# A dilated convolution on one core: all transfers on one hardware queue, no dummy matmuls, first load in halves, last stores in quarters

## The chip, the core and the metric

One core of a Trainium2 chip (trn2). The metric is the device time of the kernel in microseconds (us), as a median over several executions. Before: 127.46 us (127.44 to 127.64, 3 runs). Every ratio below compares a kernel with the kernel before, on one chip with runs of both in turn. Where two variants are set side by side, they often ran on different chips, so their ratios to before are the fairer comparison. The profiled execution of one run has its own span, which is about 1.8 us shorter than the device time (125.6 of 127.34 us before).

## The reference

A 3x3 convolution with dilation 2 over 16 images of 64 channels and 64 by 64 points, 128 output channels, all float32:

```python
batch, c_in, h, w, c_out, k, dilation = 16, 64, 64, 64, 128, 3, 2
# x_pad: zeros of width 2 around each image
for b, co, ci, kh, kw in ...:
    output[b, co] += weight[co, ci, kh, kw] * x_pad[b, ci, kh*2:kh*2+64, kw*2:kw*2+64]
```

The input is 16.8 MB, the output 33.6 MB, the weights 0.3 MB. All of it must cross between HBM and the core once.

## The kernel before

Images are handled in eight pairs (two images of 64 channels fill 128 partitions). A pair is loaded in one 2 MB transfer, cast to fp16 by ScalarE, and convolved in four groups of 16 rows. A group is 30 matmuls in three products (psP, psA, psB); ScalarE copies psP, VectorE adds it to psA and psB and writes the output tile `osb`. Each image of a pair is stored in one 2 MB transfer; those of the first and last pair in halves of 1 MB. Four input buffers and three output buffers rotate.

```python
    x32pool = ctx.enter_context(tc.tile_pool(name="x32pool", bufs=XB))     # XB = 4
    opool = ctx.enter_context(tc.tile_pool(name="opool", bufs=3))
    # ... cut
    def load(pb, rows):
        t = x32pool.tile([P, HW], f32, tag="x32", name="x32")
        x32_tiles[pb] = t
        lo = 0
        for hi in rows:
            nc.sync.dma_start(out=t[:, lo * W : hi * W], in_=x_pair[pb, :, lo * W : hi * W])
            lo = hi
    # ... cut
    def store(pb, m, lo, hi):
        queue = nc.gpsimd if pb < npairs - 1 else nc.sync
        queue.dma_start(
            out=out_img[2 * pb + m, :, lo * W : hi * W],
            in_=o_tiles[pb][:, m * HW + lo * W : m * HW + hi * W],
        )
    # ... cut
    nc.sync.dma_start(out=w32, in_=weight.rearrange("o i h w -> o (i h w)"))
    for pb in range(min(XB, npairs)):
        load(pb, [H])
    # ... cut
    run_warm(14)          # 14 dummy matmuls of 512 columns
    # ... weights: cast to wd (DVE, ACT), 15 transposes (PE), copies to w_sb (DVE, ACT)
    run_warm(14)
    # ... cut; at the end of group G = (pair pb, quarter g):
        if ahead[0] >= NG * (freed[0] + 1) and freed[0] + XB < npairs:
            load(freed[0] + XB, [H])
            freed[0] += 1
        if pb in (0, npairs - 1) and g % 2 == 1:
            for m in range(2):
                store(pb, m, (g - 1) * GR, (g + 1) * GR)
        elif 0 < pb < npairs - 1 and g == NG - 1:
            for m in range(2):
                store(pb, m, 0, H)
```

GpSimd's transfers (`nc.gpsimd`) go through the software queue, SyncE's (`nc.sync`) and ScalarE's through a hardware queue each.

## Time and profile before

| | before |
|---|---|
| device time, median | 127.46 us |
| span of the profiled execution | 125.6 us |
| TensorE (PE) dense | 10.47 to 110.5 us |
| last eviction ends (VectorE) | 111.87 us |
| last transfer fully landed | 124.48 us |
| 16 KB packet on a DMA engine, median | 611 ns |

First the page of the kernel before. In part 2, each of the 40 columns is a fortieth of the span and a digit is the busy share in tenths; in part 3, a line is a queue with its packets, megabytes and share of the 16 DMA engines' time.

```profile
span 125.6 us, 2342 instructions
...
PE   6998999999999999999979999999999999920000
...
DMA  5999999999999999999999999999999999999970
GB/s 160 383 444 418 438 423 402 381 415 444 391 457 418 410 418 436 441 444 418 423 423 425 428 449 423 428 418 423 428 449 423 428 428 418 412 431 407 428 331 16
...
q0 software_dynamic: 2304, 29.36, 55.1%
q1 hardware_dynamic: 1872, 21.27, 40.8%
q8 instruction: 8, 0.13, 0.4%
```

The DMA row is full from the second slice to the 38th. TensorE's last digit, a 2, is in slice 36, and the transfers go on into slice 39. DMA is the bound. The last slices are worth a look: 331, then 16 GB/s. Not all engines end together.

The next lines are the waits of the kernel before: engine and line, what it waited for, total us, times, longest.

```profile
DVE osb L224 <- PE psA L167: 11.7, 25, 1.1
DVE osb L224 <- DMA out_dram<-osb: 3.1, 2, 2.7
```

VectorE waited for matmuls in general, but twice, once for 2.7 us, for a store to free an output buffer. So TensorE runs ahead and DMA holds it back. The timeline of PE at the start (start, duration, work, count) shows where the dummy matmuls stand:

```profile
1.19 5.08 PE L125 MATMUL wp<-warm 128*128 128x512 f16 x14 [1.19 <-DVE warm L120]
6.11 1.00 PE L147 MATMUL wt<-ident,wd 128*128 128x128 f16 x15
6.95 3.19 PE L125 MATMUL wp<-warm 128*128 128x512 f16 x14
10.47 0.81 PE L167 MATMUL psP<-xs,w_sb 64*128 64x512 f16 x6 [0.34 <-DVE xs L98]
11.12 1.28 PE L167 MATMUL psA<-x_157,w_sb 64*128 64x512 f16 x12
...
13.49 0.80 PE L167 MATMUL psP<-xs,w_sb 64*128 64x512 f16 x6
```

The first 14 dummies take 5.08 us, the second 3.19 us: within the first set the spacing drops from 0.43 to 0.216 us at 5.0 us. The prediction reads this as TensorE's clock warming; the granted clock of that stretch is printed as 1.00 and does not show it. Last, the table of stretches of the kernel before (stretch, its length, busy time and instruction counts of PE, weight loads, DVE, ACT, POOL, then granted clock, DMA share, GB/s):

```profile
18.00:20.00 2.00, 2.00 (x22) 0.91 (x20) 1.52 (x3) 1.51 (x2) 1.20 (x2) 1.00 0.96 410
20.00:22.00 2.00, 2.00 (x22) 0.92 (x20) 1.54 (x3) 1.27 (x2) 0.00 (x0) 1.00 1.19 410
22.00:24.00 2.00, 2.00 (x24) 1.02 (x22) 1.99 (x3) 1.79 (x3) 0.00 (x0) 1.00 0.86 348
...
40.00:100.00 60.00, 59.27 (x578) 30.43 (x576) 50.98 (x58) 37.22 (x39) 4.21 (x8) 1.00 1.01 428
```

The rate is a steady 428 GB/s, except for a dip (410, then 348 GB/s).

### The profile page before, as it was taken

Reading aid. Unit: us, or ns where it says so; the run is one execution under the profiler, and the core shown is the slowest. Engines: PE = TensorE matmul, PEld = TensorE weight load, DVE = VectorE, ACT = ScalarE, POOL = GpSimd, SP = SyncE. Lnnn points to the kernel's source line nnn. Section 1 sums busy time; section 2 is a strip of 40 time slices with the busy share of each in tenths; the row PEclk is TensorE's granted clock in tenths of the full one; section 3 lists DMA queues with packets and bytes.
Section 4 is the critical chain, followed back from the end, with each engine's and each line's share of the span. In section 5 each row is a group of like instructions: output and inputs, shape, how many; then the busy total and the mean of one; then the engine's idle time right before and its main releaser. Section 6 shows DMA issues by size and latency. Waiting matters only on the chain.

```text
span 125.6 us, 2342 instructions
## 1 busy us (share of the span) xinstructions
PE 108.3 (86%) x1003; PEld 53.8 (43%) x1003; DVE 89.9 (72%) x105; ACT 66.9 (53%) x71; POOL 9.3 (7%) x22
## 2 busy tenths in 40 slices
PE   6998999999999999999979999999999999920000
PEld 2453444544454445444435555555555555500000
DVE  0732888988898888988649998889888988760000
ACT  4558686966666666666654666666666433300000
POOL 2000003030002001100210003000200120000000
PEclk9999999999999999999999999999999999997555
DMA  5999999999999999999999999999999999999970
GB/s 160 383 444 418 438 423 402 381 415 444 391 457 418 410 418 436 441 444 418 423 423 425 428 449 423 428 418 423 428 449 423 428 428 418 412 431 407 428 331 16
DMA packets 4186, 50.78 MB, mean 404 GB/s; under 512 B 464, under 2 KB 464, under 8 KB 592
## 3 DMA queue, kind: packets, MB, share of 16 engines
q0 software_dynamic: 2304, 29.36, 55.1%
q1 hardware_dynamic: 1872, 21.27, 40.8%
q8 instruction: 8, 0.13, 0.4%
q14 instruction: 2, 0.02, 0.0%
HBM read 17.07 MB, written 33.55 MB: 403 GB/s over the span
## 4 chain that ended last, share of the span: by engine, by line
PE 54%; DMA 27%; DVE 4%; DVEq 1%; ACT 1%; issue 1%; POOL 0%; SPq 0%
PE psA L167 22%; DMA out_dram<-osb 21%; PE psB L167 21%; PE psP L167 11%; DMA x_80<-in_x_dram 6%; DVE osb L224 4%; ACT x_157 L88 1%; DVEq L274 1%; DVE xs L98 1%; POOL out_dram L102 0%; SPq L111 0%; DVEq L224 0%
## 5 line engine op out<-in xcount | busy, mean ns | idle before, releaser
L167 PEld LDWEIGHTS <-w_sb 64*128 64x128 f16 x960 | 49.9, 94 | 50.6 <-issue 1.0
L220 ACT COPY p_sb<-psP 128x1024 f32<-128x1024 f32 x32 | 32.4, 1012 | 37.7 <-PE psP L167 18.2
L224 DVE TENSOR_TENSOR osb<-psA,p_sb 128x1024 f32<-128x1024 f32 x32 | 39.2, 1224 | 15.2 <-PE psA L167 11.7
L224 DVE TENSOR_TENSOR osb<-psB,p_sb 128x1024 f32<-128x1024 f32 x32 | 39.0, 1218 | 0.0
L167 PE MATMUL psP<-xs,w_sb 64*128 64x496 f16 (+1 forms) x192 | 25.7, 371 | 0.3 <-DVE xs L98 0.3
L102 POOL DMA_DIRECT2D out_dram<-osb x16 | 8.6, 540 | 91.3 <-DVE osb L224 91.3
L125 PE MATMUL wp<-warm 128*128 128x512 f16 x28 | 8.3, 460 | 1.2 <-DVE warm L120 1.2
L167 PE MATMUL psB<-x_695,w_sb 64*128 64x496 f16 (+3 forms) x48 | 5.6, 365 | 0.7 <-DVE osb L224 0.7
L167 PE MATMUL psB<-x_1017,w_sb 64*128 64x496 f16 (+3 forms) x48 | 5.6, 365 | 0.0
L167 PE MATMUL psB<-x_856,w_sb 64*128 64x496 f16 (+3 forms) x48 | 5.6, 365 | 0.0
L167 PE MATMUL psB<-x_1178,w_sb 64*128 64x496 f16 (+3 forms) x48 | 5.6, 365 | 0.0
L167 PE MATMUL psA<-x_1178,w_sb 64*128 64x496 f16 (+3 forms) x48 | 5.6, 365 | 0.0
L167 PE MATMUL psA<-x_1017,w_sb 64*128 64x496 f16 (+3 forms) x48 | 5.6, 365 | 0.0
L167 PE MATMUL psA<-x_856,w_sb 64*128 64x496 f16 (+3 forms) x48 | 5.6, 365 | 0.0
L167 PE MATMUL psA<-x_695,w_sb 64*128 64x496 f16 (+3 forms) x48 | 5.6, 365 | 0.0
L167 PE MATMUL psA<-x_157,w_sb 64*128 64x496 f16 (+3 forms) x48 | 5.6, 365 | 0.0
L167 PE MATMUL psA<-x_240,w_sb 64*128 64x496 f16 (+3 forms) x48 | 5.6, 365 | 0.0
L167 PE MATMUL psA<-x_532,w_sb 64*128 64x496 f16 (+3 forms) x48 | 5.6, 365 | 0.0
L167 PE MATMUL psA<-x_369,w_sb 64*128 64x496 f16 (+3 forms) x48 | 5.6, 365 | 0.0
L167 PE MATMUL psB<-x_240,w_sb 64*128 64x496 f16 (+3 forms) x48 | 5.6, 365 | 0.0
L167 PE MATMUL psB<-x_157,w_sb 64*128 64x496 f16 (+3 forms) x48 | 5.6, 365 | 0.0
L167 PE MATMUL psB<-x_369,w_sb 64*128 64x496 f16 (+3 forms) x48 | 5.6, 365 | 0.0
(35 smaller groups left out, 66.3 us busy)
## 6 DMA issues: line engine op xcount, KB each, us to landing
out_dram<-osb POOLq DMA_DIRECT2D x12, 2048.0 KB, 17.6
out_dram<-osb POOLq DMA_DIRECT2D x4, 1024.0 KB, 20.8
out_dram<-osb SPq DMA_DIRECT2D x4, 1024.0 KB, 11.8
x_80<-in_x_dram SPq DMA_DIRECT2D x1, 2048.0 KB, 7.6
x_82<-in_x_dram SPq DMA_DIRECT2D x1, 2048.0 KB, 12.0
x_84<-in_x_dram SPq DMA_DIRECT2D x1, 2048.0 KB, 17.9
x_86<-in_x_dram SPq DMA_DIRECT2D x1, 2048.0 KB, 23.8
x_245<-in_x_dram SPq DMA_DIRECT2D x1, 2048.0 KB, 17.5
```

Source lines behind the costliest of these rows:

```text
L88: nc.scalar.copy(out=x16_tiles[pb][:, lo * W : hi * W], in_=x32_tiles[pb][:, lo * W : hi * W])
L98: nc.vector.tensor_tensor(out=s, in0=v[:, :, 0], in1=v[:, :, 1], op=add)
L102: queue.dma_start(out=out_img[2 * pb + m, :, lo * W : hi * W], in_=o_tiles[pb][:, m * HW + lo * W : m * HW + hi * W],)
L125: nc.tensor.matmul(out=wp[:, 0:512], lhsT=warm[:, 0:P], rhs=warm)
L167: nc.tensor.matmul(out=po, lhsT=w_sb[pp, t * CO : (t + 1) * CO], rhs=rhs, start=first and j == 1, stop=last and j == 2,)
L220: nc.scalar.copy(out=p_sb, in_=psP)
L224: nc.vector.tensor_tensor(out=o[:, :, b0 : b0 + NBLK, e], in0=ps.rearrange("p (m b q) -> p m b q", m=2, q=2 * W), in1=pv, op=add,)
L274: with _tile.TileContext(nc) as tc:
```

## The change

The intent: one kind of queue, with transfers in the order of the program; no work on TensorE that isn't needed; an earlier start of the first cast; a shorter last transfer.

```diff
     def store(pb, m, lo, hi):
-        queue = nc.gpsimd if pb < npairs - 1 else nc.sync
-        queue.dma_start(
+        nc.sync.dma_start(
 ...
     for pb in range(min(XB, npairs)):
-        load(pb, [H])
+        load(pb, [H] if pb else [32 + d, H])
 ...
-    warm = wpool.tile([P, 512], f16, name="warm")
-    nc.vector.memset(warm, 0.0)
-    (definition of run_warm cut)
-    run_warm(14)
 ...
-    run_warm(14)
 ...
-        if pb in (0, npairs - 1) and g % 2 == 1:
+        if pb == npairs - 1 and g == NG - 1:
+            for m in range(2):
+                for lo in (2 * GR, 3 * GR):
+                    store(pb, m, lo, lo + GR)
+        elif pb in (0, npairs - 1) and g % 2 == 1:
```

More of the change, by code (lines that the diff above doesn't have):

```diff
@@ L112 @@
     for pb in range(min(XB, npairs)):
-        load(pb, [H])
+        load(pb, [H] if pb else [32 + d, H])
     ident = wpool.tile([P, P], f16, name="ident")
     make_identity(nc, ident)
-    warm = wpool.tile([P, 512], f16, name="warm")
-    nc.vector.memset(warm, 0.0)
-    wp = ppool.tile([P, 1024], f32, tag="p", name="wp")
-    def run_warm(n):
-        for _ in range(n):
-            nc.tensor.matmul(out=wp[:, 0:512], lhsT=warm[:, 0:P], rhs=warm)
-    run_warm(14)
     KINDS = 5
```

## The prediction

> **What bounds it now.** The DMA engines. The page's DMA row shows 9 in 37 of 40 slices; the table of stretches gives 428 GB/s from 40 to 100 us. 17.07 MB read plus 33.55 MB written at that rate is 118 us (estimate) of the 125.6 us span. TensorE is dense from 10.47 to 110.5 us, a group of 30 matmuls every 3.17 us. The chain of waits calls PE 54%, but at 64.4 us VectorE has waited 2.67 us for a store to free an output buffer: PE is ahead and DMA holds it back.
>
> Landings differ by engine: of the last store half the increments had come at 122.5 us, the last at 124.48. The instruction queue fetches 8 packets of 16 KB, one per 13 us; I think all on one engine. It moves (50.62/16 + 0.131) MB; at 611 ns per 16 KB this is 122.9 us (estimate), from its first packet at 1.74 us to 124.6: never idle, the true bound.
>
> **What the change does.**
> 1. *Stores to the hardware queue.* The Trainium skill ("DMA: Bandwidth & Descriptors", "Issuing engines are not separate DMA queues") says queues share the same 16 engines; the trace agrees: 426 GB/s with the hardware queue alone (9 to 18.7 us), 428 with the software queue alone (80 to 100 us). No gain in rate. Order changes to first in, first out: pair 1's stores land near 58 us, not 64.4, and the output-buffer wait (0.9 us of PE) disappears.
> 2. *No dummy matmuls.* 28 matmuls, 8.3 us of PE, all in its free time. But they warm the clock: the first ran at 0.43 us spacing until 5.0 us, the second 14 at 0.228. The skill ("TensorE: Matmul & The Clock Gate", Part 1) puts the half clock at the first 3.4 us of activity; this trace shows about 3.8. Now transposes run cold (1.6 us, not 1.0), and the first 4 to 5 us of real matmuls cost double: PE about 2.4 us late (1.7 to 3.5). Net of step 1, PE's work ends about 113.4 instead of 111.9.
> 3. *Half first load.* Lands near 6 us instead of 8.78, but the cast follows ScalarE's weight copies, which now end near 8.9. Worth nothing.
> 4. *Quarter stores.* One goes 3.2 us earlier, behind work still queued. Nothing.
> 5. PE's program is 56 instructions shorter: at 256 per fetch, the fetch at 111.47 us should not occur: 0.6 us less for the slowest engine.
>
> **Critical path.** Does PE's lateness starve DMA? At 100.1 us, when pair 6's stores are issued, the preceding store still needs 2.8 us on the median engine, 4.5 on the slowest. 1.5 us later plus 1 us to first data just fits: median engines idle 0 to 1 us, the slowest never. So only the 0.6 us reaches the end.
>
> **Prediction: 126.9 us, range 125.6 to 128.6.** Faster by over 2%: 0.06; within 2%: 0.88; slower: 0.06.
>
> **What would show it.** DMA row 9 throughout; first real matmuls at doubled spacing until about 15 us; first group near 10.6; no long wait of VectorE for stores; last eviction near 113.4; 7 instruction fetches; last landing near 123.9.
>
> **What would make it wrong.** The clock staying low longer, so that DMA idles before pair 6's stores (slower); alternation of two queues itself costing time (348 GB/s at 22 to 24 us, as the software queue starts), so that one queue saves 1 to 2 us; the hardware queue blocking its issuer (its two-store issues took 1.25 and 1.90 us).

## The result, and the profile after

The changed kernel took 127.63 us (median of 6 runs, 127.56 to 127.70), the kernel before 127.45 us in the same rounds. The ratio is 1.0013, 95% interval 1.0000 to 1.0026. (Ratios here are the mean time of one kernel's fast runs over that of the other's of the same rounds, so not quite the ratio of the medians.) Executions over 1.5% slower than the fastest of the same kernel are left out of the means. The time lies inside the predicted range and within 2%, but the gain of 0.6 us that was forecast did not come; if anything, 0.2 us were lost.

The page of the changed kernel:

```profile
span 125.8 us, 2289 instructions
...
PE   0519999999999999999999999999999999930000
...
DMA  4999999999999999999999999999999999999980
GB/s 135 391 458 432 417 427 432 443 284 414 453 427 396 450 424 417 432 435 437 406 422 427 424 443 427 417 432 432 427 437 427 422 417 427 448 409 411 413 326 35
...
q1 hardware_dynamic: 4608, 50.63, 96.2%
q8 instruction: 7, 0.11, 0.3%
```

One queue, still full throughout, and seven instruction fetches instead of eight, as forecast. VectorE's waits in the changed kernel:

```profile
DVE osb L211 <- PE psA L155: 14.4, 26, 2.9
DVE osb L211 <- ACT p_sb L207: 1.6, 5, 0.6
DVE osb L211 <- PE psB L155: 0.4, 1, 0.4
```

These are all of its waits at the eviction: there is none for a store any more. The start of PE in the changed kernel:

```profile
4.39 0.50 PE L135 MATMUL wt<-ident,wd 128*128 128x128 f16 x3 [4.39 <-DVE wd L123]
5.21 1.65 PE L135 MATMUL wt<-ident,wd 128*128 128x128 f16 x12 [0.32 <-DVE wd L126]
9.63 1.43 PE L155 MATMUL psP<-xs,w_sb 64*128 64x512 f16 x6 [2.78 <-DVE xs L98]
10.84 2.42 PE L155 MATMUL psA<-x_127,w_sb 64*128 64x512 f16 x12
13.03 2.24 PE L155 MATMUL psB<-x_127,w_sb 64*128 64x512 f16 x12
15.10 0.81 PE L155 MATMUL psP<-xs,w_sb 64*128 64x512 f16 x6
```

The real work begins 0.84 us earlier than before, its first group is slow (1.43, 2.42 and 2.24 us for the three products; later ones take 0.81, 1.44 and 1.44), and the second group starts 1.6 us later than before (15.10 against 13.49). The last eviction ends at 112.57 us, 0.7 us later than before. The stretches of the changed kernel:

```profile
24.00:26.00 2.00, 2.00 (x24) 1.16 (x22) 2.00 (x3) 1.79 (x3) 0.00 (x0) 1.00 1.01 418
26.00:28.00 2.00, 2.00 (x24) 1.08 (x20) 1.83 (x4) 1.40 (x2) 0.00 (x0) 1.00 1.04 270
28.00:30.00 2.00, 2.00 (x22) 0.96 (x18) 1.52 (x3) 1.65 (x2) 0.00 (x0) 1.00 0.86 352
...
40.00:100.00 60.00, 60.00 (x585) 31.20 (x582) 52.15 (x60) 37.52 (x39) 0.00 (x0) 1.00 1.01 428
```

The same 428 GB/s from 40 to 100 us; the dip has moved to 26 to 30 us and is deeper.

No view above tells why the end did not move. A finer reading does. The Trainium skill ("DMA: Bandwidth & Descriptors", "Why a DMA increments its semaphore by 16 and not by 1") says that each of the 16 engines adds one to the semaphore when its own share has landed. The trace keeps the time of each of these 16 updates, so for each transfer it shows when the median engine was done and when the last one was. I worked out the following from those times (us from the start of the span; "late" is the last engine minus the median):

```
                                first store of pair 2       last store
kernel                          median   last   late      median    last   late
before                           67.80  69.22   1.43      122.51  124.48   1.98
after                            67.95  70.97   3.01      122.61  125.02   2.41
```

The median engine is the same to 0.15 us in both kernels. What differs is how late the last engine is, and in both it is about two us late at the end. So the question is what makes single engines late.

### The profile page after: what moved, and what is told of

Same layout as the page of the kernel before. It is cut to its first block, busy times and chain, and to the rows that moved or that the text cites. A ratio compares the mean times of both kernels' runs of the same rounds, so it can differ in the third digit from the quotient of the medians.

```text
span 125.8 us, 2289 instructions
## 1 busy us (share of the span) xinstructions
PE 103.7 (82%) x975; PEld 53.7 (43%) x975; DVE 90.0 (72%) x104; ACT 66.9 (53%) x71; POOL 0.7 (1%) x6
## 4 chain that ended last, share of the span: by engine, by line
PE 81%; DVE 3%; DMA 2%; ACT 1%; DVEq 1%; issue 0%
PE psA L155 32%; PE psB L155 31%; PE psP L155 17%; DMA w_78<-in_weight_dram 2%; PE wt L135 1%; DVE osb L211 1%; DVEq L265 1%; ACT x_127 L88 1%; DVE wd L126 1%; DVE wd L123 1%; ACT w_sb L142 0%; DVE w_sb L141 0%; DVE xs L98 0%; DVEq L211 0%
## 5 line engine op out<-in xcount | busy, mean ns | idle before, releaser
L155 PEld LDWEIGHTS <-w_sb 64*128 64x128 f16 x960 | 52.3, 95 | 51.9 <-issue 5.2
L155 PE MATMUL psP<-xs,w_sb 64*128 64x496 f16 (+1 forms) x192 | 26.5, 379 | 2.8 <-DVE xs L98 2.8
L155 PE MATMUL psA<-x_127,w_sb 64*128 64x496 f16 (+3 forms) x48 | 6.7, 420 | 0.0
L155 PE MATMUL psB<-x_127,w_sb 64*128 64x496 f16 (+3 forms) x48 | 6.4, 403 | 0.0
L135 PE MATMUL wt<-ident,wd 128*128 128x128 f16 x15 | 2.1, 308 | 4.7 <-DVE wd L123 4.4
L155 PE MATMUL psB<-x_339,w_sb 64*128 64x496 f16 (+3 forms) x48 | 5.6, 365 | 0.0
L155 PE MATMUL psB<-x_502,w_sb 64*128 64x496 f16 (+3 forms) x48 | 5.6, 365 | 0.0
L155 PE MATMUL psB<-x_826,w_sb 64*128 64x496 f16 (+3 forms) x48 | 5.6, 365 | 0.0
L155 PE MATMUL psB<-x_210,w_sb 64*128 64x496 f16 (+3 forms) x48 | 5.6, 365 | 0.0
L155 PE MATMUL psB<-x_665,w_sb 64*128 64x496 f16 (+3 forms) x48 | 5.6, 365 | 0.0
L155 PE MATMUL psB<-x_987,w_sb 64*128 64x496 f16 (+3 forms) x48 | 5.6, 365 | 0.0
L155 PE MATMUL psB<-x_1148,w_sb 64*128 64x496 f16 (+3 forms) x48 | 5.6, 365 | 0.0
L155 PE MATMUL psA<-x_339,w_sb 64*128 64x496 f16 (+3 forms) x48 | 5.6, 365 | 0.0
L155 PE MATMUL psA<-x_502,w_sb 64*128 64x496 f16 (+3 forms) x48 | 5.6, 365 | 0.0
L155 PE MATMUL psA<-x_826,w_sb 64*128 64x496 f16 (+3 forms) x48 | 5.6, 365 | 0.0
L155 PE MATMUL psA<-x_987,w_sb 64*128 64x496 f16 (+3 forms) x48 | 5.6, 365 | 0.0
L155 PE MATMUL psA<-x_210,w_sb 64*128 64x496 f16 (+3 forms) x48 | 5.6, 365 | 0.0
L155 PE MATMUL psA<-x_665,w_sb 64*128 64x496 f16 (+3 forms) x48 | 5.6, 365 | 0.0
L155 PE MATMUL psA<-x_1148,w_sb 64*128 64x496 f16 (+3 forms) x48 | 5.6, 365 | 0.0
```

The costliest lines, as they stand in the source:

```text
L135: nc.tensor.matmul(out=wt[:, (t - q) * CO : (t - q + 1) * CO], lhsT=wd[:, t * 2 * CI : (t + 1) * 2 * CI], rhs=ident,)
L155: nc.tensor.matmul(out=po, lhsT=w_sb[pp, t * CO : (t + 1) * CO], rhs=rhs, start=first and j == 1, stop=last and j == 2,)
```

## The experiments

Two theories at first. **B**, the prediction's: the queues are alike, one engine takes all instruction fetches and ends last, so fewer fetches shorten the end. **A**: fetches fall on different engines and delay each its own; the slow engine comes from the software queue; in one queue, lateness from before 40 us stays to the end; the two effects cancel. Later theories are named where they arise. Eighteen runs were made, one of them a repeat, all with correct results except two that were wrong. Each trace is of one execution; the repeat (y0 of x3c) shows how far two traces of one kernel differ: 0.5 us in the last landing at 68 us, 0.2 us in the last of all.

### One part of the change at a time

**e1_hwstores**: before, with only `store` on `nc.sync`:

```diff
-        queue = nc.gpsimd if pb < npairs - 1 else nc.sync
-        queue.dma_start(
+        nc.sync.dma_start(
```

> Only the stores move to the hardware queue. Theory A (two effects cancel): the one engine that was 5% slow while only the software queue ran (its landings 5.1 us apart instead of 4.86) now keeps pace, which is worth about 1 us; but in one first-in-first-out queue the delays of single engines from before 40 us stay to the end, and the slow stretch before the first store is about 0.4 us longer. Net within 0.4 us of before, spread of the last landing about 2.4 us over the median. Theory B (of the prediction: queues alike, only instruction fetches count; still 8 of them): same time as before, within 0.2 us, and the engine with the last landing is late by the same 2.0 us for the same reason, the fetches.

Measured: 127.95 us against 127.44, ratio 1.0031 (1.0018 to 1.0044). By the ratio this is 0.4 us, at the edge of theory A and outside theory B's 0.2. The last engine was 2.75 us late in the last store.

**e2_nowarm**: before, without the `warm` tile and both `run_warm(14)`.

> Only the 28 dummy matmuls go; 7 instruction fetches instead of 8. Theory B (all fetches on one engine, which ends last): 0.6 us faster than before. Theory A (fetches fall on different engines, each delays only its own): within 0.2 us of before. Both: the transposes start near 4.4 us, because they stood behind the dummy matmuls; the first real matmul then follows the first load (lands near 8.8 us), so near 10.5 us.

Measured: 127.7 us, ratio 1.0016 (1.0003 to 1.0029). Seven fetches, and no gain: theory B fails here. One of the six executions, the profiled one, took 628.3 us and, apart from the number of fetches, is used for nothing above or below. What it showed is told at the end.

**e3_half**: before, with `load(pb, [H] if pb else [32 + d, H])`.

> Only the first load in halves. Both theories: the end is set by DMA, so no change within 0.2 us; the first real matmul about 0.2 us earlier, because the weight copies end at 8.56 us against the landing at 8.78.

Measured: 127.41 us, ratio 1.0002 (0.9989 to 1.0015). No effect.

**e4_quarters**: before, with the last half images stored in quarters.

> Only the last half images in quarters. Both theories: within 0.2 us of before; the slowest engine still has work queued when the quarters are issued. Four smaller transfers could cost up to 0.1 us in extra packets.

Measured: 127.5 us, ratio 0.9997 (0.9985 to 1.0009). No effect.

So the queue is the only part that moves the time clearly, by 0.4 us for the worse; the missing dummies cost 0.2 us, at the edge of the noise.

### One part taken back, more fetches, a first-store test, a second hardware queue

**e5_all_but_hw**: the changed kernel with the old queue line in `store`.

> The changed kernel with the stores of pairs 0 to 6 back on the software queue. Theory A (delays of single engines, which stay to the end in one queue and are partly made good while two queues run, against the software queue's one slow engine): between before and the changed kernel, so ratio to before 0.999 to 1.002; the slow engine's landings again 5.1 us apart in the store-only phase; lateness of the last engine at 63 us below 2 us. Theory B (queues alike, all fetches on one engine): 0.6 us faster than before, as the changed kernel should have been.

Measured: 127.43 us, ratio 1.0004 (0.9992 to 1.0016). Again seven fetches without the 0.6 us of theory B. The last engine's landings were 5.1 us apart in the store-only phase, and 69.70 us at the first store of pair 2.

**x2_more_pe**: the changed kernel, with more instructions on TensorE while it is idle:

```diff
+    for _ in range(128):
+        nc.tensor.matmul(out=tp[:, 0:32], lhsT=tw[:, 0:P], rhs=tw[:, 0:32])
     KINDS = 5
```

> The changed kernel with 128 tiny matmuls (256 more instructions on TensorE) in its idle start: one instruction fetch more (8 instead of 7), and each fetch about 256 instructions earlier. Theory B: 0.6 us slower than the changed kernel. Theory A: within 0.3 us of the changed kernel, and the engine that the first fetch delays is again late by about 1.0 to 1.4 us from that moment, to the end.

Measured: 127.8 us, ratio to before 1.0037 (1.0012 to 1.0062), where the changed kernel had 1.0013. By time alone this lies between the theories. By the trace it is theory A: eight fetches, the first at 6.74 us, and the last landing at 125.01 us, against 125.02 with seven. The early fetch also moved the lateness of one engine: the last engine is 1.24 us behind the median at 8.8 us, where the changed kernel, whose first fetch is at 20.98 us, has 0.55 until 18.3 us and 1.60 at 23.2 us.

**x1_touch**: the changed kernel with a small store ahead of the first load, to see whether the dip before the first store belongs to the first store as such:

```diff
+    touch = wpool.tile([P, 64], f32, name="touch")
+    nc.vector.memset(touch, 0.0)
+    nc.sync.dma_start(out=out_img[0, :, 0:64], in_=touch)
     for pb in range(min(XB, npairs)):
```

> The changed kernel with one small store (128 rows of 256 bytes, overwritten later by the real one) ahead of the first load. Theory C (the slow 2 us before the first store's data, in which packets of 611 ns take about 1,000, belong to the first store of the program, whatever stands around it): the slow stretch at 25 to 28 us vanishes or shrinks to less than half (0.8 us mean over the engines now), and a part shows at the start instead; up to 0.5 us faster than the changed kernel. Rival (it belongs to the change from long loads to long stores): the stretch at 25 to 28 us stays at 0.6 to 0.9 us.

Measured: 128.45 us, ratio 1.0102 (1.0057 to 1.0147). Packets in the stretch from 26 to 28 us still took 0.84 us per engine more than their usual time (0.81 in the changed kernel), so theory C falls. Three engines were about 1.9 us late from the first load on, but that is not what set the end, where the last engine is 2.46 us late (2.41 in the changed kernel). What moved the end is the median engine: it is 0.56 us behind the changed kernel's already at 18 us, and 0.67 us at the end (123.28 against 122.61 us).

**x3_store_act**: the changed kernel with `nc.scalar.dma_start` in `store`.

> The changed kernel with all stores on the second hardware queue, issued from ScalarE: two queues again, but no software queue. If the software queue itself makes one engine slow (5.1 us between its landings in the store-only phase), then here all engines keep 4.86 us there. If sharing between two queues is what makes good the late engines between 31 and 63 us, then the last engine's lateness at 63 us is below 2 us as in before; if it is the software queue, it stays near 3 us as in the changed kernel. Time: if both hold, 0.5 to 1 us faster than before; else equal to the changed kernel within 0.3 us. ScalarE pays about 0.4 to 1 us for each of 22 issues, which it has idle.

Measured: 132.45 us, ratio 1.0402 (1.0368 to 1.0435). A miss, and a plain one: in ScalarE's program each store now stands before its next copy, so a store that waits for VectorE holds that copy up too. The DMA row of the page of x3_store_act, then a line of its waits:

```profile
DMA  4999999999999999999999999999369945999995
```

```profile
DVE osb L213 <- ACT p_sb L209: 20.2, 9, 2.8
```

VectorE now waits 20.2 us for ScalarE, where it waited 1.6, and DMA runs dry near the end (the digits 3, 6, 4, 5). It says nothing about two hardware queues. The next set does.

### Two queues or one, hardware or software

The later loads depend only on ScalarE's own casts, so ScalarE can issue those without waiting for anybody.

**x3c_loads_act**: the changed kernel, with

```diff
-            load(freed[0] + XB, [H])
+            load(freed[0] + XB, [H], nc.scalar)    # load() takes the queue, nc.sync if none
```

> The changed kernel, but the four later loads are issued from ScalarE's hardware queue, where they wait only for ScalarE's own casts; stores stay on SyncE's hardware queue. Two hardware queues, no software queue, nothing that starves DMA. If two queues are what keeps the late engines less late (theory A), the last engine's landing for the first store of pair 2 is near 69.4 us, as with the software queue, not near 71.0; and with no software queue the store-only phase has no engine at 5.1 us per 2 MB. Then the last landing is near 123.5 us and the kernel about 1% faster than before (126.2 us). If the software queue itself is what keeps them less late, the last engine stays near 71 us and the time is that of the changed kernel, 127.6.

Measured: 127.39 us, ratio 0.9969 (0.9934 to 1.0004) beside a kernel before that was noisy on this chip (127.32 to 128.79). Repeated as **y0_loads_act_again** on another chip:

> The changed kernel with its later loads on ScalarE's hardware queue, run again as the base of this set. Engine A is early again (about 69.3 us at the first store of pair 2), engine S sets the end: 127.3 to 127.6 us, within 0.2 us of before.

Measured: 127.53 us, ratio 1.0007 (0.9994 to 1.0020). So it equals before; the 1% did not come.

**x3d_loads_act_warm**: the same two queues put into the kernel before.

> The kernel before (dummy matmuls, whole first load, half-image stores) with only the queues of the run above: all stores on SyncE's hardware queue, the four later loads on ScalarE's. Same two outcomes: about 126.2 us if two queues are what helps and the software queue what hurts; about 127.9, as with the stores alone moved, if not. If it equals the run above within 0.2 us, dummy matmuls, half load and quarters are worth nothing here either.

Measured: 127.62 us, ratio 0.9983 (0.9948 to 1.0019). As before.

**x4_all_sw**: the changed kernel with `nc.gpsimd` for every transfer.

> The changed kernel with every transfer on the one software queue: one queue, but not the hardware one. If the long slow stretch before the first store (0.65 to 0.85 us mean over the engines in one hardware queue, 0.4 to 0.6 with two) and the 71 us of the last engine belong to one queue, they show here too. If one engine is slow whenever the software queue feeds it, it is slow from the first load, 5% of some 118 us: the last landing near 130 us and the time near 132 us. If it is slow only in stores, near 128.5 us.

Measured: 130.58 us, ratio 1.0208 (1.0167 to 1.0249). Between the two forecasts: its first data move at 2.68 us instead of 1.74, and the last engine is 3.6 us late at the end. An engine that is slow by 5% from the first load would have given 132.

**e6_all_but_nowarm**: the changed kernel with the dummies kept.

> The changed kernel with the dummy matmuls kept; 8 instruction fetches again. Theory B: 0.6 us slower than the changed kernel. Theory A: within 0.2 us of it. TensorE's real work starts near 10.2 us at full speed and its last eviction comes about 1 us before that of the changed kernel, without effect on the end.

Measured: 127.64 us, where the changed kernel had 127.63 on another chip; ratio to the noisy before of its own chip 0.9995 (0.9958 to 1.0032). Eight fetches, last landing 124.91 us. Theory B wanted 0.6 us more than the changed kernel, a ratio near 1.006.

Put together, from the times of the 16 updates (us):

```
                                          first store of pair 2      last store
kernel              queues                median   last   late     median    last
before              2, stores software     67.80  69.22   1.43     122.51  124.48
e5_all_but_hw       2, stores software     68.32  69.70   1.38     122.51  124.92
x3c_loads_act       2, both hardware       68.05  69.29   1.24     122.40  124.71
x3d_loads_act_warm  2, both hardware       68.03  69.52   1.49     122.52  124.90
after               1, hardware            67.95  70.97   3.01     122.61  125.02
e1_hwstores         1, hardware            67.92  70.89   2.97     122.35  125.10
e6_all_but_nowarm   1, hardware            68.61  71.27   2.67     123.18  124.91
x4_all_sw           1, software            69.31  72.69   3.37     123.98  127.55
```

Two readings. First, it is one queue against two, not hardware against software, that decides how late the last engine is at 68 us: about 1.4 us with two queues, about 3 with one. That part of theory A is shown. (x1, one queue, is only 1.68 us late there because its median engine is late as well; its last landing, 71.04 us, is that of one queue.) Second, most of the gain of 1.5 us with two queues is gone at the end, with two hardware queues too: the last landings lie between 124.48 and 125.10 us with one hardware queue or two of any kind. In x3c the last landings of the 2 MB stores from 79 to 110 us are 5.06 to 5.16 us apart, without any software queue; eight packets of 611 ns are 4.89. So an engine that slowly falls behind exists there as well, and theory A's blame on the software queue falls.

The packets confirm this. Of the 16 KB packets that start between 68 and 100 us, about one in 16 takes near 644 ns instead of 611 in every one of these kernels:

```
kernel             packets of 16 KB   of these 624 to 700 ns   their median
before                   833                  50                 644 ns
after                    835                  49                 644 ns
x3c_loads_act            836                  50                 644 ns
```

One in 16 is one engine's share (the trace does not name the engine; that it is one engine is inferred from this share and from the steady growth of one lateness). Call it S. It loses 8 x 33 ns = 0.26 us in each 2 MB store. In the loads no engine is slow in this way: of the 237 packets of 16 KB that start between 9 and 18 us in the changed kernel, none. In the changed kernel's single queue S is still about 1.4 us ahead of the last engine at 78 us, and reaches it only near 103 us, where the two latest engines are 2.23 and 2.27 us behind the median. At the last store they are 2.41 and 2.01 us late. So in the changed kernel two engines end late by about the same amount for different reasons, and to cut one alone is worth at most the 0.4 us between them. In the kernel before, S is alone: 1.98 us late, the next engine 0.78.

### Is S slow because of 16 KB packets?

Three kernels store every pair, or pairs 4 to 7, in half images (8 KB packets).

**y1_after_halves**: `store` of all pairs at `g % 2 == 1`, otherwise the changed kernel.

> The changed kernel with all stores in half images, so 8 KB packets (309 ns) instead of 16 KB (611): 12 x 2 MB of stores cost each engine 0.056 us more per 2 MB, 0.67 us in all (estimate from the packet times). If engine S is slow only in 16 KB store packets, no packet is slow by 5% any more; but engine A, late in the one queue, sets the end: 0.3 to 0.8 us slower than the changed kernel, about 128.2 us. Rival: S is slow in every store; then one packet in 16 still takes about 5% longer (324 ns instead of 309).

Measured: 128.88 us, ratio 1.0114 (1.0099 to 1.0129).

**y2_act_some_halves** and **y3_act_halves**: on top of y0.

> y0 with the stores of pairs 4 to 7 in half images, pairs 1 to 3 whole: engine S loses 6 x 0.26 us less, all engines pay 6 x 0.056 = 0.34 us. If the end is the later of A and S, and both are now cut, last landing 0.5 to 0.9 us earlier than in y0: about 126.7 us, faster than before by 0.5%. If neither sets the end, 0.3 us slower than y0.

> y0 with all stores in half images: S has no 16 KB store left; all engines pay 0.67 us. If the end is the later of A and S: between y2 and y0, about 127.0 us. If neither: 0.6 us slower than y0.

Measured: y2 127.81 us, ratio 1.0041 (1.0020 to 1.0061); y3 128.26 us, ratio 1.0065 (1.0051 to 1.0080); y0 of the same set 1.0007. All three are slower, y2 and y3 by about the estimated cost of smaller packets (0.34 and 0.67 us) and y1 by more. By its last landing (125.68 us, against 125.02) y1 too loses the estimate; the rest of its time lies after that landing and was not looked into. In y3, 87 of 1,858 packets of 8 KB between 68 and 104 us took 322 to 350 ns (median 309). So S is slow in stores of either packet size, the rival that y1 named, and smaller packets only cost.

### The transfers alone, and the transfers beside TensorE

**z1_dma_only** issues exactly the changed kernel's transfers, in its order and sizes, from three zeroed tiles, with no other work. Its result is wrong.

> Wrong result on purpose (the output is zeros): the changed kernel's transfers, same sizes, order and queue, with no arithmetic but three memsets, so no waits on compute and no instruction fetch of TensorE. If engines fall behind because of fetches and compute, all 16 increments of the last store come within 0.7 us of each other, and the last landing is near 122.3 us (that of the changed kernel's median engine, less 0.3): a time near 124.7 us. If the transfers alone make single engines late, the last increment is again about 2 us after the median and the time about 127.

**z2_dma_and_pe** adds 960 matmuls on constant data that nothing waits for. Wrong too.

> z1 plus 960 matmuls of 512 columns on constant data, which nothing waits for: TensorE busy for about 100 us, with 7 instruction fetches, but no VectorE or ScalarE work. If fetches delay single engines, their steps of 1.0 to 1.4 us for one engine are back, last landing 1 to 1.5 us later than in z1. If engine S is slow because of TensorE, one packet in 16 takes about 644 ns again; if not, none.

Measured: z1 125.97 us (125.1 to 127.18), ratio 0.99 (0.9858 to 0.9942). z2 135.16 us, ratio 1.0612 (1.0584 to 1.0640), but that time is not one of DMA: I had put the matmuls' constant tile behind 20 us of memsets, so TensorE started at 27 us and ended after the transfers. Only z2's transfers are read here. Part 3 of the page of z1:

```profile
DMA packets 4608, 50.63 MB, mean 411 GB/s; under 512 B 512, under 2 KB 512, under 8 KB 1280
...
q1 hardware_dynamic: 4608, 50.63, 97.7%
```

And of z2, where the line of the instruction queue is back:

```profile
q1 hardware_dynamic: 4608, 50.63, 90.7%
q8 instruction: 7, 0.11, 0.3%
```

The landings and the packets between 68 and 100 us:

```
                  last store               16 KB packets   of these 624 to 700 ns
kernel          median    last   late
z1_dma_only     121.77  122.52   0.75           841                 0
z2_dma_and_pe   122.36  124.93   2.57           836                50
after           122.61  125.02   2.41           835                49
```

This settles, for these traces, what makes engines late at the end: TensorE's running. Without it no packet of the 841 is slow and no engine lands more than 0.76 us after the median; with it, and with no ScalarE work, no VectorE work after 27 us and no waits, the end is back where the changed kernel has it. Both kinds of lateness return. The fetches: z2's first fetch is at 40.47 us, and the lateness of the last engine goes from 0.62 us (a transfer at 39.4) to 2.09 (the next, at 43.4). That the fetch packet itself does it rests on this timing, on x2, and on the one engine that falls behind right after the first fetch in the kernel before and the changed one (0.32 to 1.72 and 0.54 to 1.60 us). And S: 50 slow packets, one in 16, with a median of 636 ns.

Two limits. The traced execution of z1 was the fastest of its six (125.10 us; the other fast ones went up to 126.58), and why the others took longer without TensorE is not known. And a fetch is not all of the first late engine's lateness: in the changed kernel it goes from 1.60 to 2.59 us between the landings at 23 and 29 us, in the dip, with no fetch in between.

None of the eighteen runs beat both kernels: those within noise of before are e3, e4, e5, x3c with its repeat y0, x3d and e6, and the only one that was faster, z1, does not compute the result. z1 gains 1% by its time and 2.5 us by the last landing of its fastest execution. By z2, which has TensorE's running and otherwise only transfers and lands last at 124.93 us, 2.4 us of these are what TensorE's running costs, most of it (1.8 us) through the lateness of single engines.

## Why the prediction was right or wrong

*What bounds the kernel.* Right that it is DMA: z1, the transfers alone, has its median engine done at 121.77 us, against 122.61 in the changed kernel. Right that the engine that ends last sets the time. **Wrong in why it is last: "I think all on one engine". This is the step that failed.** The prediction gave all eight fetches to one engine (122.9 us of work from 1.74 us on), and the sum met the landing at 124.48 us by chance. In the runs, fetches delay different engines (in the changed kernel three separate engines are each 1.0 to 1.4 us later after the first, second and third), and another engine, S, falls behind by 0.26 us per 2 MB store while TensorE runs. In the kernel before the last engine is S from about 83 us on: its lateness grows store by store from 1.21 to 2.19 us, and the fetch at 111.47 us, the one to be saved, adds nothing to it (2.19 us in the last store before that fetch; 2.18, 2.00, 1.96 and 1.98 in the four last transfers).

*Step 5, one fetch less, 0.6 us.* The fetch did disappear (7 instead of 8). The gain did not: e2 and e5 have seven fetches and ratios of 1.0016 and 1.0004; x2 and e6 have eight and the last landing of seven to 0.1 us. The size of the term was 0.6 us predicted, 0 measured. The count was right: between two fetches of the kernel before TensorE starts 227 to 288 instructions, 256 on average.

*Step 1, the queue.* The rate is the same, as said (428 GB/s in both kernels). The Trainium skill's statement that queues share the same engines holds. Pair 1's stores landed at 58.25 us on the median engine (predicted near 58) and 60.74 on the last, and the output-buffer wait vanished, as said. What was missed: one queue leaves the last engine 1.5 us later at 68 us than two queues do. By the end S has used up most of that with two queues, so at the end only 0.4 us (e1) to 0.2 us (the whole change) remain as a loss. Why two queues leave the late engines less late is not settled. The dip before the first store is deeper in one queue (packet times add up to an excess of 0.65 to 0.84 us per engine, against about 0.3 to 0.6 with two queues), which may be a part of it.

*Step 2, the dummies.* Right that they are off the critical path and that the first group runs at half speed: doubled spacing until about 14.7 us. Wrong in their place: the transposes had been standing behind the dummies, so they move from 6.11 to 4.39 us and the real work starts earlier (9.63 us, predicted near 10.6). The delay of TensorE was 1.6 us instead of 2.4. The order of instructions before showed this: transposes that begin where the dummies end were not waiting for weights.

*Step 3, the half load.* Worth nothing for the end, as said, but for another reason: with the dummies gone the cast starts at 7.97 us, before the whole load would have landed (9.06 us). It let TensorE start about 1.1 us earlier (estimate from these two times), off the critical path.

*Step 4, the quarters.* Right: e4 is at 0.9997.

*The critical path.* Right that TensorE's lateness is absorbed: its last eviction came 0.7 us later than before (112.57 us; predicted 113.4), and the rate of DMA shows no gap before pair 6's stores.

## What to carry to other kernels

When a kernel is bound by DMA, look at the 16 updates of each transfer before explaining its end: the median engine and the last one can be 2 us apart, and only the last one counts. Before crediting a saving to the last engine, check that the saving falls on that engine; two engines that are late by much the same for different reasons make each remedy nearly worthless alone. And a measurement of the transfers by themselves, beside one of the transfers with a single engine running, tells in two runs what a dozen variants of the kernel do not.

## What the Trainium skill lacked or had wrong

- "Runtime: NRT & Kernel Launch", "Instruction fetch mechanics", says that engines fetch instructions in 16 KiB blocks of 256 instructions over their own DMA queue, at a cost that is mostly hidden. The trace agrees on size and rhythm (one 16 KB packet per 12.6 to 14.6 us in the kernels before and after). It lacks what a fetch costs the transfers beside it: the packet takes 879 to 1,039 ns, and after z2's first fetch the last engine's lateness rose by 1.47 us. Whether that reaches the end depends on which engine ends last; here one fetch less gained nothing.
- "DMA: Bandwidth & Descriptors", "Latency and other measured facts", says that two of the engines are usually slower and guesses that this is specific to the software queue. Here one engine's share of store packets is slow (644 instead of 611 ns) in kernels without any software transfer too (after, x3c), and in none when TensorE does not run (0 of 841 packets in z1). The traces do not name the engines, so whether it is one of those two stays open, as does what TensorE and that engine share.
- The same page, "Issuing engines are not separate DMA queues", says that more issuers only save issue time. For the rate this holds (428 GB/s each way). It lacks that the lateness of single engines at 68 us was about 1.4 us with two queues and 3 us with one.
- No page that I read has the dip before the first stores: for some 2 us many packets of 611 ns take about 1,000 to 1,200, in z1 too, 0.3 to 0.84 us per engine over the kernels. A small earlier store did not remove it (x1).
- "TensorE: Matmul & The Clock Gate", Part 1, puts the half clock at the first 3.4 us of activity, with a switch around 4 us, give or take 0.5. Here the dummies ran at 0.43 us spacing for 3.8 us, which agrees, and the first real group at reduced speed for about 5 us (9.63 to 14.68 us), which is longer. The page also warns of TensorE stuck at a low rate for over 50 us. One execution of e2, a kernel without dummies, looks like such a state for its whole 626 us, by its groups (matmuls of 365 ns in other runs):

```profile
L158 PE MATMUL psB<-x,w_sb 64*128 64x496 f16 (+3 forms) x384 | 255.6, 1642 | 0.0
L158 PE MATMUL psP<-xs,w_sb 64*128 64x496 f16 (+1 forms) x192 | 138.5, 1674 | 2.8 <-DVE xs L98 2.8
```

  The granted clock printed for it is 1.00 all along, so that column did not show it. None of the other executions of this or of the other kernels here without dummies did the same, and the cause was not looked for.
